# State-space stage of a two-layer backbone: phase sums and modulation weights moved to other stages, cosine in three steps, another order in the loop

## The chip, the core and the metric

The kernel runs on one core of a Trainium2 chip. The core has five engines that work side by side, each through its own list of instructions in order: TensorE (PE; loading of its weights is PEld), VectorE (DVE), ScalarE (ACT), GpSimd (POOL) and SyncE (SP). In this kernel SP issues every DMA transfer, so all transfers stand in one list. The metric is the time of one execution on the device, in microseconds (us).

## The reference

Two layers over 1024 latent tokens and 256 context tokens of width 1024, in float32. Layer 0 mixes tokens by differential attention, layer 1 by a bidirectional diagonal complex state-space recurrence (S5) with a GLU. A squared-ReLU MLP follows each mixer. Every sub-layer is normalized, and shifted, scaled and gated by "modulation" vectors: the product of SiLU(c) with a weight matrix of 1024 x 6144 for each layer, cut into six segments.

```python
def s5_scan(u, lam_bar, b_bar, c_mat, h0):              # per direction, 64 groups of 16 channels, 64 states
    ...
        bu = jnp.einsum('gpc,btgc->btgp', b_bar, uc.astype(jnp.complex64))
        a_cum, hs = lax.associative_scan(_linear_combine, (a, bu), axis=1)
        hs = hs + a_cum * h[:, None]
        y = jnp.real(jnp.einsum('gcp,btgp->btgc', c_mat, hs))
...
    def glu(y, h):
        g = jax.nn.gelu(y.astype(h.dtype))
        o1, o2 = jnp.split(jnp.einsum('btd,de->bte', g, w_glu), 2, axis=-1)
        return o1 * jax.nn.sigmoid(o2)
...
        mod_l = (jnp.einsum('bd,de->be', sc, ada_w[i]) + ada_b[i])[:, None, :]
        sh1, s1, g1, sh2, s2, g2 = jnp.split(mod_l, 6, axis=-1)
```

## The kernel before

Products that need float32 precision are made of three passes with split operands (`mm3`, L130 to L134: high by high, high by low, low by high), so most of the TensorE time stands on lines 132, 133 and 134. `split` (L136) makes the halves: ScalarE copies the high part, another engine subtracts for the low part. `dma` (L79) puts each transfer on SP.

In most stages a scheduler of the library sets the order of each engine's instructions and of SP's transfers, by its own estimate of times. Inside `manual` (L583) the order of PE, DVE, ACT and POOL is the program's own; SP's is still the scheduler's.

The stages that matter here, with their place in the profile:

- **First stage** (`phase_v`, L337, to about 245 us): modulation of layer 0, the V projection and the start of the K and Q projections. Beside it run, interleaved step by step, the remaining modulation segments of layer 0 (`ada`, products on L202) and `s5_prep` (L950), which prepares the state-space parameters. `s5_prep` also makes one phase step per state and direction, as a 32-bit integer turn, and stores it to DRAM (`phd`, L1018).
- **MLP of layer 0, second product** (`mlp0_down`, L1581): `s5_phases` (L1199) runs beside it. From the phase steps it fills by repeated doubling a fine table (16 positions) and a coarse table (10 positions of 16), and stores both (`ptd`).
- **State-space stage** (`s5`, L1735, about 1876 to 2101 us): 16 periods n, each for four channel groups in both directions d, over 160 positions at a time. A period's steps, all in `manual` order:
  - `phase` (L1773): POOL adds coarse and fine table to 640 integer phases (L1777).
  - `trig` (L1779): ScalarE makes sine and cosine. The cosine takes the sine of half the angle, a square, and a copy with scale -2 and bias 1: four instructions with the sine.
  - `inputs` (L1790, PE on L1797), `rotate` (L1799, two DVE multiplies on L1806), a POOL sum of both (L1887 or L1896), `scan` (L1813, on L1815), `back` (L1817, on L1823: one product on DVE, one on POOL), `outputs` (L1825, PE on L1829 and L1832).
  - the GELU two periods later (L1870 to L1904), and transposes of its result (`tr`, L1834), split in `tr_out` (L1838: the low half is L1841 on DVE).
  - eight half segments of layer 1's modulation: weights of 2 MB each are loaded into memory that the stage has freed, and multiplied in periods 8, 10 and 12 to 17 (`ada_half_products`, products on L247).
- **GLU** (`glu`, L1929, about 2102 to 2330 us): two groups g of four token tiles; for each of four column blocks nb, eight weight transfers and four tiles of 24 matmuls.

Three PSUM regions are shared by the input products of both directions, so that each product waits for the rotation of the third product before it. The outputs of a period are written to one of two banks, from which the GELU reads, and which the transposes then overwrite.

Of the kernel before, what the change touches and what calls it, by code (L numbers as in the profile page):

```python
# [70 lines left out]
class Prog:  # L71
# [265 lines left out]
    def phase_v(self):  # L337
# [48 lines left out]
        self.bg = [self.interleave([self.ada(0, seg, acc) for seg in (2, 3, 4)] + [self.rows_out(0, acc)],  # L386
# [15 lines left out]
        for nb in range(2):  # L402
            for n, (g, i) in enumerate(tok[4 * (1 - nb) :]):
# [16 lines left out]
                self.step(6 if nb and n else 7)  # L420
# [529 lines left out]
    def s5_prep(self):  # L950
# [67 lines left out]
        self.dma(self.phd, pc)  # L1018
# [180 lines left out]
    def s5_phases(self, o):  # L1199
# [3 lines left out]
        B, P, P16 = (self.fv(x, *d).bitcast(I32) for x, d in ((o, (128, 16)), (o + 8, (128,)), (o + 8.5, (128,))))  # L1203
        self.dma(self.fv(o + 9, 128), self.phd)
        nc.vector.tensor_copy(P, self.fv(o + 9, 128))
# [11 lines left out]
        fill(B, 16, P)  # L1217
        g(P16, B[:, :, 8], B[:, :, 8], ALU.add)
        self.dma(self.ptd[:, 5 * KB : 13 * KB], B.rearrange("p a b -> p (a b)"))
        yield  # L1220
        A = self.fv(o, 128, 10).bitcast(I32)
        fill(A, 10, P16)
        self.dma(self.ptd[:, 0 : 5 * KB], A.rearrange("p a b -> p (a b)"))
        yield
# [356 lines left out]
    def mlp0_down(self):  # L1581
# [6 lines left out]
        self.bg = [self.s5_phases(40), self.s5_tables(0, self.bank(3), self.bank(2))]  # L1588
# [146 lines left out]
    def s5(self):  # L1735
# [10 lines left out]
        At, Bt = self.fv(42.5, 128, 10).bitcast(I32), self.fv(47.5, 128, 16).bitcast(I32)  # L1746
        A0, B0 = self.hv(46, 2, 4, 10).bitcast(I32), self.hv(47, 2, 4, 16).bitcast(I32)
        phs = [(self.fv(x, 4, 160), self.fv(x + 2.5, 4, 160)) for x in (0, 7.5, 24.5)]
        ts = [[(self.fv(x, 4, 160), self.fv((12.5, 20)[d], 4, 160)) for x in ((5, 29.5), (15, 17.5))[d]] for d in range(2)]
# [9 lines left out]

        mods = [(6, 8), (8, 10), (10, 12), (11, 13), (12, 14), (13, 15), (14, 16), (15, 17)]  # L1760
        halves = [[self.view(self.U, 16 * i + 4 * kk, (2, 512)) for kk in range(4)] for i in range(2)]
# [11 lines left out]
        def phase(n, d):  # L1773

            x0, P = 64 * d + 4 * n, phs[(2 * n + d) % 3][0].bitcast(I32)
            a, b = (At[:, x0 : x0 + 4], Bt[:, x0 : x0 + 4]) if n else (A0[:, d], B0[:, d])
            pool.tensor_tensor(P.rearrange("p x (a b) -> p x a b", b=16), bcast(a, 3, 16), bcast(b, 2, 10), ALU.add)  # L1777

        def trig(n, d):  # L1779
            Ps, Pc = phs[(2 * n + d) % 3]  # L1780
# [3 lines left out]
            act.activation(Pc, Pc, AF.Copy, scale=-2.0, bias=1.0)  # L1784
# [14 lines left out]
        def rotate(n, d):  # L1799
            (Ps, Pc), (t1, t2) = phs[(2 * n + d) % 3], ts[d][n % 2]  # L1800
# [16 lines left out]
        def back(eng, n, d, j):  # L1817
            Ps, Pc = phs[(2 * n + d) % 3]
# [4 lines left out]
            eng.tensor_tensor(o, ts[d][n % 2][1][:, :, h], (Ps if j else Pc)[:, :, h], ALU.mult)  # L1823
# [19 lines left out]
        for t, c0, w in ((A0, 0, 10), (B0, 5 * KB, 16)):  # L1843
            self.dma(t, self.ptd[:, c0 : c0 + 128 * w].rearrange("p (d x w) -> p d x w", d=2, w=w)[:, :, 0:4])

        load_x(0)
        self.dma(self.fv(42.5, 13 * KB).bitcast(I32), self.ptd)
        load_w(0)
        self.act_set("silu_and_others")
        with self.manual():  # L1850
            act.activation(U[:, :, 160:192], U[:, :, 0:32], AF.Copy)
            for d in range(2):
                for i in range(2):
                    pool.memset(rs[d][i][:, :, 0:1], 0.0)
            phase(0, 0)
            phase(0, 1)
# [4 lines left out]
            for n in range(19):  # L1861
                run, m = n < 16, n - 2
                gelu = 0 <= m < 16
# [3 lines left out]
                if 1 <= n <= 16:  # L1867
                    back(pool, n - 1, 1, 1)
# [6 lines left out]
                if 0 < n < 15:  # L1875
                    phase(n + 1, 0)
                if run:
                    rotate(n, 0)
                if lo:
                    lo()  # L1880
                if gelu:
                    v.scalar_tensor_tensor(u, u, 1.0, y, ALU.add, ALU.mult)
                    act.activation(u, u, AF.Tanh, scale=float(np.sqrt(2.0 / np.pi)))
                if run:
                    inputs(n, 1)
                    t1, t2 = ts[0][n % 2]
                    pool.tensor_tensor(t1, t1, t2, ALU.add)  # L1887
                if gelu:
                    act.activation(u, u, AF.Copy, bias=1.0)
                if 0 < n < 15:  # L1890
                    trig(n + 1, 0)
                    decay(n + 1, 0)
                if run:
                    rotate(n, 1)
                    t1, t2 = ts[1][n % 2]
                    pool.tensor_tensor(t1, t1, t2, ALU.add)  # L1896
                    scan(n, 0)
                    if n == 0:
                        phase(1, 0)
                        trig(1, 0)  # L1900
                        decay(1, 0)
# [3 lines left out]
                if run:  # L1905
                    back(v, n, 0, 0)
                    back(pool, n, 0, 1)
                    scan(n, 1)
                    back(v, n, 1, 0)
                if 1 <= n <= 16:  # L1910
                    outputs(n - 1)
# [394 lines left out]
```

## Time and profile before

| what | us |
|---|---|
| runs of the kernel before | 2925.51, 2938.06, 2945.19 |
| their median | 2938.06 |
| span of the profiled execution, first to last instruction | 2929.2 |

The profiled execution has no time of its own beside its span; the median of the runs is 8.9 us above that span.

| stretch of the profile, us | PE busy | DVE | ACT | POOL | DMA share |
|---|---|---|---|---|---|
| 0 to 245, first stage | 205.96 | 113.54 | 74.18 | 54.06 | 0.81 |
| 1500 to 1870, MLP of layer 0 | 357.37 | 278.70 | 155.78 | 53.07 | 0.84 |
| 1870 to 1905, start of the state-space stage | 10.24 | 24.14 | 14.27 | 17.36 | 0.62 |
| 2075 to 2100, its end | 19.48 | 16.33 | 8.49 | 7.59 | 0.95 |

How to read the lines below: in a timeline a row gives start, duration, engine, source line, operation, output <- input, shape, and in brackets the idle time ahead of it with what ended it. SPq is SP's list of transfers. In a group of instructions stand the busy time, the mean of one in ns, and the idle time before them. Durations of matmuls overlap; what one costs is the step from one to the next.

### The profile page before, as it was taken

To read this page: it belongs to the slowest core of one execution; us is meant where nothing else is said; L and a number is where in the kernel's file an instruction comes from. 1 tells how busy PE (TensorE), PEld (TensorE's weight loads), DVE (VectorE), ACT (ScalarE), POOL (GpSimd) and SP (SyncE) were. 2 spreads that over 40 slices of the span, in tenths; PEclk is the share of its full clock that TensorE was granted. 3 is DMA by queue.
4 is the path that set the end of the run, shared out by engine and by line. 5 is a ranking of instruction groups with operands and counts; after the bars stand their busy time and mean duration, and the time that the engine had idled before them with its cause. 6 is when DMAs were issued, how large, how long until landed. Compare 5 with 4: busy or idle time off the path is not lost.

```text
span 2929.2 us, 43646 instructions
## 1 busy us (share of the span) xinstructions
PE 2739.6 (94%) x15200; PEld 2287.5 (78%) x15200; DVE 2021.3 (69%) x2956; ACT 1367.5 (47%) x2555; POOL 1062.1 (36%) x923
## 2 busy tenths in 40 slices
PE   5998999999988999999999999688899899999999
PEld 3687888788777887878877778588788678878887
DVE  5355777777764477676688768699743687758566
ACT  3424555555553663333444435377543643345443
POOL 2213666666553700000020004499410543326324
PEclk8999999999989999999999999899999999999999
DMA  9956455555744448886699988468834254467544
GB/s 250 292 181 205 139 164 169 162 149 162 220 145 152 140 152 303 303 291 243 228 299 293 274 241 258 153 200 264 282 124 136 72 175 159 148 213 256 159 139 141
DMA packets 454122, 588.44 MB, mean 201 GB/s; under 512 B 62742, under 2 KB 299532, under 8 KB 450700
## 3 DMA queue, kind: packets, MB, share of 16 engines
q1 hardware_dynamic: 453900, 585.63, 63.6%
q8 instruction: 120, 1.97, 0.3%
q14 instruction: 102, 0.84, 0.1%
HBM read 398.48 MB, written 182.82 MB: 198 GB/s over the span
## 4 chain that ended last, share of the span: by engine, by line
PE 66%; DMA 12%; DVE 10%; issue 4%; ACT 4%; SPq 2%; POOL 2%; DVEq 0%; ACTq 0%; POOLq 0%
PE PS L132 19%; PE PS L133 18%; PE PS L134 18%; SPq L80 2%; PE PS L520 2%; PE PS L1797 2%; ACT F L543 2%; PE PS L1832 1%; PE PS L566 1%; DVE F L533 1%; DVE R L138 1%; DVE H L138 1%; PE PS L202 1%; DMA U<-in_mlp_w 1%; DMA U<-Aa 1%
## 5 line engine op out<-in xcount | busy, mean ns | idle before, releaser
L132 PE MATMUL PS<-H 128*128 128x512 f32 x1048 | 412.0, 395 | 7.7 <-DVE FD L1604 5.0
L133 PE MATMUL PS<-H 128*128 128x512 f32 x1048 | 410.4, 392 | 0.0
L134 PE MATMUL PS<-H 128*128 128x512 f32 x1048 | 409.8, 392 | 0.0
L132 PE MATMUL PS<-H,R 128*128 128x512 f32 (+1 forms) x836 | 311.2, 378 | 18.5 <-ACT F L579 13.7
L133 PE MATMUL PS<-H,R 128*128 128x512 f32 (+1 forms) x836 | 303.8, 363 | 1.1 <-POOL H L138 1.1
L134 PE MATMUL PS<-H,R 128*128 128x512 f32 (+1 forms) x836 | 303.6, 364 | 0.0
L137 ACT ACTIVATE R<-W 128x512 fp32r<-128x512 f32 (+1 forms) x203 | 142.9, 711 | 208.7 <-PE PS L133 114.9
L132 PEld LDWEIGHTS PS<-H 128*128 128x128 f32 x1048 | 197.9, 189 | 52.4 <-DVE FD L1604 5.3
L134 PEld LDWEIGHTS PS<-H 128*128 128x128 f32 x1048 | 197.7, 189 | 42.5 <-issue 1.0
L133 PEld LDWEIGHTS PS<-H 128*128 128x128 f32 x1048 | 197.9, 189 | 41.2 <-issue 1.2
L132 PE MATMUL PS<-R,H 128*128 128x512 f32 x532 | 214.7, 407 | 7.4 <-ACT H L137 6.0
L543 ACT ACTIVATE F<-F,stat 128x1280 f32<-128x1280 f32 x128 | 174.3, 1362 | 83.8 <-DVE F L533 83.5
L133 PE MATMUL PS<-R,H 128*128 128x512 f32 x532 | 210.8, 397 | 0.0
L134 PE MATMUL PS<-R,H 128*128 128x512 f32 x532 | 208.3, 395 | 0.0
L137 ACT ACTIVATE H<-U 128x640 fp32r<-128x640 f32 x216 | 132.8, 677 | 144.2 <-PE PS L133 110.7
L132 PEld LDWEIGHTS PS<-H,R 128*128 128x128 f32 x836 | 160.7, 193 | 47.6 <-ACT F L579 15.1
L138 DVE TENSOR_TENSOR H<-W,H 128x512 fp32r<-128x512 f32 (+1 forms) x137 | 128.6, 949 | 93.6 <-ACT H L137 93.6
L138 DVE TENSOR_TENSOR R<-W,R 128x512 fp32r<-128x512 f32 (+1 forms) x166 | 150.8, 915 | 60.8 <-ACT R L137 53.5
L533 DVE TENSOR_SCALAR_CACHE_REDUCE F<-PS 128x1280 f32<-128x1280 f32 x128 | 185.1, 1482 | 9.1 <-PE PS L520 8.9
L138 DVE TENSOR_TENSOR H<-U,H 128x640 fp32r<-128x640 f32 x216 | 163.4, 793 | 39.5 <-ACT H L137 39.3
L580 POOL TENSOR_SCALAR R<-F 128x256 fp32r<-128x256 f32 (+1 forms) x128 | 122.8, 959 | 172.1 <-ACT F L579 149.1
L134 PEld LDWEIGHTS PS<-H,R 128*128 128x128 f32 x836 | 160.7, 192 | 25.9 <-issue 0.8
(477 smaller groups left out, 6818.0 us busy)
## 6 DMA issues: line engine op xcount, KB each, us to landing
W<-in_mlp_w SPq DMA_DIRECT2D x184, 256.0 KB, 3.1
U<-Aa SPq DMA_DIRECT2D x108, 320.0 KB, 5.0
Aa<-FU SPq DMA_DIRECT2D x91, 320.0 KB, 4.6
Ad<-F SPq DMA_DIRECT2D x112, 256.0 KB, 3.2
W<-Ad SPq DMA_DIRECT2D x112, 256.0 KB, 2.8
W<-in_ada_w SPq DMA_DIRECT2D x32, 512.0 KB, 6.9
FU<-in_mlp_w SPq DMA_DIRECT2D x32, 512.0 KB, 6.3
Ta<-FU SPq DMA_DIRECT2D x16, 1024.0 KB, 5.6
```

Of the source, the lines that this page charges most:

```text
L80: return self.nc.sync.dma_start(out=out, in_=in_)
L132: mm(out, ah, bh, start=first, stop=False, **kw)
L133: mm(out, ah, bl, start=False, stop=False, **kw)
L134: mm(out, al, bh, start=False, stop=last, **kw)
L137: self.nc.scalar.activation(hi, src, AF.Copy)
L138: (lo_eng or self.nc.vector).tensor_tensor(lo, src, hi.bitcast(F32), ALU.subtract)
L202: self.nc.tensor.matmul(acc[32 * j : 32 * j + 32, 0:256], self.scT[:, 2 * k : 2 * k + 32], w[:, 256 * j : 256 * j + 256], start=k == 0, st ...
L520: mm(self.PS[:, 1280 * c + k0 : 1280 * c + k1], Q[:, c, r, qs], K[c][:, k0:k1], start=r == 0, stop=r == 1)
L533: ts(p[c], self.PS[:, 1280 * c : 1280 * c + 1280], 1.0, None, ALU.mult, ALU.min, accum_out=sm[:, c : c + 1])
L543: nc.scalar.activation(p[c], p[c], AF.Exp, bias=sm[:, c : c + 1], scale=-1.0, accum_out=sn[:, 0:1] if c else s0[:, u + 1 : u + 2])
L580: nc.gpsimd.tensor_scalar(hi, t, 1.0, 0.0, ALU.mult, ALU.add)
L1797: mm(b[:, o : o + 160], X[:, d, i, 64 * j : 64 * j + 128], U[:, 4 * n + i, cols], start=True, stop=True)
```

## The change

Four edits.

1. `s5_phases` moves to the first stage, behind layer 0's modulation in the interleaved list, with memory of its own (`PH`, 14.75 KB per partition). It takes the phase steps from there, and not from DRAM, fills the tables for each direction, and adds them for all 16 periods: 32 sums of 128x640 on POOL, each stored to DRAM. The stage takes ten background steps where it took seven. In the state-space stage `phase` becomes a load of 320 KB; the two tables are not loaded any more.
2. The cosine is the sine of a quarter turn minus the absolute phase: with the sine three ScalarE instructions.
3. The order in a period: the scan of direction 1 moves behind the next period's first rotation, with its two products; POOL's sums, the low half and the GELU steps move with it. Phases have five buffers in place of three.
4. Layer 1's eight modulation halves leave the state-space loop. Each is multiplied in the GLU's first group after every second tile, from one set of four buffers that is loaded again after each; the modulation rows are written out after the second and the eighth.

```diff
-        self.bg = [self.interleave([self.ada(0, seg, acc) for seg in (2, 3, 4)] + [self.rows_out(0, acc)],
+        self.bg = [self.interleave([self.ada(0, seg, acc) for seg in (2, 3, 4)] + [self.rows_out(0, acc), self.s5_phases()],
...
-                self.step(6 if nb and n else 7)
+                self.step(10 if nb and n else 7)
...
-        self.dma(self.phd, pc)
+        v.tensor_copy(self.view(self.PH, 0, (128,)).bitcast(I32), pc)
...
+        out = Ring([i32(7.25 + 2.5 * i, 4, 10, 16) for i in range(3)])
...
+        for d in range(2):
+            fill(B, 16, P[:, 64 * d : 64 * d + 64])
+            g(P16, B[:, :, 8], B[:, :, 8], ALU.add)
+            fill(A, 10, P16)
+            yield
+            for n in range(16):
+                t, x = out.next(), slice(4 * n, 4 * n + 4)
+                g(t, bcast(A[:, x], 3, 16), bcast(B[:, x], 2, 10), ALU.add)
+                self.dma(self.phd[2 * n + d], t.rearrange("p x a b -> p (x a b)"))
+                yield
...
-        self.bg = [self.s5_phases(40), self.s5_tables(0, self.bank(3), self.bank(2))]
+        self.bg = [self.s5_tables(0, self.bank(3), self.bank(2))]
...
         def phase(n, d):
-            x0, P = 64 * d + 4 * n, phs[(2 * n + d) % 3][0].bitcast(I32)
-            a, b = (At[:, x0 : x0 + 4], Bt[:, x0 : x0 + 4]) if n else (A0[:, d], B0[:, d])
-            pool.tensor_tensor(P.rearrange("p x (a b) -> p x a b", b=16), bcast(a, 3, 16), bcast(b, 2, 10), ALU.add)
+            self.dma(phs[(2 * n + d) % 5][0].bitcast(I32).rearrange("p x n -> p (x n)"), self.phd[2 * n + d])
...
-            act.activation(Pc, Ps.bitcast(I32), AF.Sin, scale=0.5 * UNPHASE)
+            act.activation(Pc, Ps.bitcast(I32), AF.Abs, scale=UNPHASE)
             act.activation(Ps, Ps.bitcast(I32), AF.Sin, scale=UNPHASE)
-            act.activation(Pc, Pc, AF.Square)
-            act.activation(Pc, Pc, AF.Copy, scale=-2.0, bias=1.0)
+            act.activation(Pc, Pc, AF.Sin, scale=-1.0, bias=quarter)
```

The loop's new order, without its conditions (n is the period, m = n - 2 the one whose GELU is made):

```python
hi(n); square(m); trig(n, 1); decay(n, 1); inputs(n, 0); rotate(n, 0); decay(n + 1, 0)
scan(n - 1, 1); back(v, n - 1, 1, 0); back(pool, n - 1, 1, 1); add(n, 0); phase(n + 2, 0)
lo(); gelu step, tanh, plus 1; inputs(n, 1); rotate(n, 1); trig(n + 1, 0); outputs(n - 1)
scan(n, 0); back(v, n, 0, 0); back(pool, n, 0, 1); add(n, 1); gelu product
tr; phase(n + 2, 1); load_x(n + 2); load_w(n + 1)
```

And in the GLU:

```diff
-        for _ in self.rows_out(1, self.bank(3)):
-            pass
-        self.row_bc(G, 1, 2, 0)
+        halves = [(seg, h) for seg in (2, 3, 4, 5) for h in range(2)]
+        hw = [self.fv(16 + 4 * i, 2, 512) for i in range(4)]
+        self.ada_half_load(hw, 1, *halves[0])
...
+                    if g == 0 and t % 2:
+                        i = 2 * nb + t // 2
+                        self.ada_half_products(hw, 1, *halves[i], self.bank(5)[:, 0:128])
+                        if i < 7:
+                            self.ada_half_load(hw, 1, *halves[i + 1])
+                        if i in (1, 7):
+                            for _ in self.rows_out(1, self.bank(3)):
+                                pass
+                        if i == 1:
+                            self.row_bc(G, 1, 2, 0)
```

More of the change, by code (lines that the diff above doesn't have):

```diff
@@ L1745, in s5 @@
         rs = [[self.view(self.U, 52 + 5 * d + 2.5 * i, (4, 160)) for i in range(2)] for d in range(2)]
[L1746 to L1749, printed above, removed]
+        phs = [(self.fv(x, 4, 160), self.fv(x + 2.5, 4, 160)) for x in (0, 42.5, 7.5, 47.5, 24.5)]
+        quarter = self.fv(52.5, 1)
+        ts = [[(self.fv(x, 4, 160), self.fv(y, 4, 160)) for x, y in p]
+              for p in (((5, 12.5), (29.5, 53)), ((15, 20), (17.5, 20)))]
         cs = [[(self.fv(x, 4, 128), self.fv(y, 4, 128)) for x, y in (((5, 32), (29.5, 34)), ((15, 22.5), (17.5, 22.5)))[d]]
@@ L1874, in s5 @@
                     inputs(n, 0)
-                if 0 < n < 15:
-                    phase(n + 1, 0)
+                    rotate(n, 0)
+                if n + 1 < 16:
+                    decay(n + 1, 0)
+                if last:
+                    scan(n - 1, 1)
+                    back(v, n - 1, 1, 0)
+                    back(pool, n - 1, 1, 1)
                 if run:
-                    rotate(n, 0)
+                    add(n, 0)
+                if n + 2 < 16:
+                    phase(n + 2, 0)
                 if lo:
```

83 lines of the change are left out of this document (27 added, 56 removed).

## The prediction

> **What bounds the kernel now.** I read the page first, then the busy time by stretches, then one period of the state-space loop in order of time.
>
> ```profile
> span 2929.2 us, 43646 instructions
> ...
> PE 66%; DMA 12%; DVE 10%; issue 4%; ACT 4%; SPq 2%; POOL 2%; DVEq 0%; ACTq 0%; POOLq 0%
> ```
>
> TensorE carries two thirds of the chain that ended last. So matmuls added to a stage in which TensorE is full cost their whole length, and work on other engines counts only where TensorE waits for it. The stretches tell which stage is which (columns: PE, PEld, DVE, ACT, POOL busy, granted clock, DMA share, GB/s):
>
> ```profile
> 120.00:140.00 20.00, 19.98 (x138) 13.77 (x138) 8.52 (x12) 11.26 (x18) 2.88 (x4) 1.00 0.94 315
> 140.00:160.00 20.00, 20.00 (x116) 15.31 (x115) 8.74 (x10) 3.85 (x7) 3.78 (x3) 1.00 1.05 362
> 160.00:180.00 20.00, 20.00 (x103) 16.78 (x102) 7.20 (x15) 5.39 (x10) 1.69 (x3) 1.00 0.18 51
> 180.00:200.00 20.00, 20.00 (x109) 17.09 (x108) 17.15 (x50) 4.22 (x9) 4.31 (x4) 1.00 0.64 211
> 220.00:240.00 20.00, 12.84 (x66) 10.88 (x64) 2.95 (x5) 2.10 (x4) 1.29 (x1) 0.81 0.96 302
> ...
> 1905.00:2075.00 170.00, 149.94 (x1378) 143.57 (x1379) 164.26 (x160) 128.34 (x203) 160.25 (x87) 0.96 0.81 245
> ...
> 2100.00:2330.00 230.00, 218.70 (x973) 178.81 (x972) 104.82 (x123) 107.29 (x191) 50.31 (x51) 0.98 0.39 126
> ```
>
> The first stage (to 245) is full on TensorE with POOL nearly empty. The loop of the state-space stage (1905 to 2075) is the only place where DVE (164 of 170) and POOL (160) are full and TensorE is not. The GLU (2100 to 2330) is TensorE again, 95%, with DMA at 0.39. The change takes work from the second of these and puts it into the first and the third.
>
> **One period of the loop.** The two low halves (L1841) of neighbouring groups, 11.54 us apart, bracket a period without modulation:
>
> ```profile
> 1955.05 0.67 DVE L1841 SCALAR_TENSOR_TENSOR H<-PS,H 128x512 fp32r<-128x512 f32 x1
> ...
> 1955.64 0.67 DVE L1882 SCALAR_TENSOR_TENSOR FD<-FD,PS 128x512 f32<-128x512 f32 x1
> ...
> 1956.11 1.55 POOL L1887 TENSOR_TENSOR FD<-FD 128x640 f32<-128x640 f32 x1
> 1956.24 1.54 DVE L1806 TENSOR_TENSOR FD<-PS,FD 128x640 f32<-128x640 f32 x2
> ...
> 1957.70 1.49 DVE L1815 TENSOR_TENSOR_SCAN FD<-U,FD 128x640 f32<-128x640 f32 x1
> ...
> 1959.11 0.66 DVE L1904 TENSOR_TENSOR FD<-FD,PS 128x512 f32<-128x512 f32 x1
> ...
> 1960.34 0.60 PE L1836 MATMUL PS<-ident,FD 128*128 128x128 f32 x4
> ...
> 1960.78 3.43 PE L1797 MATMUL PS<-U,H 128*128 128x160 f32 x24
> 1961.02 2.56 DVE L1815 TENSOR_TENSOR_SCAN FD<-U,FD 128x640 f32<-128x640 f32 x1
> ...
> 1966.59 0.67 DVE L1841 SCALAR_TENSOR_TENSOR H<-PS,H 128x512 fp32r<-128x512 f32 x1
> ```
>
> The same scan takes 1.49 us and 2.56 us: the second starts while a POOL sum or product over SBUF is running. So DVE's full lane is partly waiting for POOL, and a POOL instruction taken away gives time to both.
>
> **Part 1: the loop.** Rows for the sum: the first rotations of groups 0, 1 and 15, of 8 and 9, the tail's pair of products, and the first GLU matmul.
>
> ```profile
> 1893.91 0.82 DVE L1806 TENSOR_TENSOR FD<-PS,FD 128x640 f32<-128x640 f32 x1 [0.82 <-PE PS L1797]
> 1905.99 1.56 DVE L1806 TENSOR_TENSOR FD<-PS,FD 128x640 f32<-128x640 f32 x2
> ...
> 1988.19 1.54 DVE L1806 TENSOR_TENSOR FD<-PS,FD 128x640 f32<-128x640 f32 x2
> ...
> 1999.63 4.51 PE L1797 MATMUL PS<-U,W 128*128 128x160 f32 x32
> 2000.99 0.82 DVE L1806 TENSOR_TENSOR FD<-PS,FD 128x640 f32<-128x640 f32 x1
> 2002.08 0.82 DVE L1806 TENSOR_TENSOR FD<-PS,FD 128x640 f32<-128x640 f32 x1 [0.26 <-PE PS L1797]
> ...
> 2074.93 1.55 DVE L1806 TENSOR_TENSOR FD<-PS,FD 128x640 f32<-128x640 f32 x2
> ...
> 2084.95 0.69 DVE L1823 TENSOR_TENSOR FD<-FD 128x512 f32<-128x512 f32 x1
> 2085.08 1.69 POOL L1823 TENSOR_TENSOR FD<-FD 128x512 f32<-128x512 f32 x1 [1.52 <-DVE FD L1815]
> ...
> 2102.94 2.08 PE L132 MATMUL PS<-R,H 128*128 128x512 f32 x4 [1.42 <-ACT R L137]
> ```
>
> From 1893.91 to 2074.93 the fifteen periods take 181.0. Removed: two POOL sums of phases per period. But the new order closes another ring. DVE now does rotation (n,0), scan (n-1,1), product, low half, GELU step, rotation (n,1), scan (n,0), product, GELU product; only then may TensorE transpose, since the transposes overwrite the bank that the GELU product reads; and the next group's input products stand behind the transposes. Measured from one rotation's start: its second multiply comes 1.09 later (2000.99 to 2002.08) and frees DVE after 0.73 (half of 1956.24 to 1957.70), 1.82; scan 1.49, 3.31; product 0.69, 4.00; low half and GELU step 0.59 and 0.60 (issue to issue, 1955.05, 1955.64, 1956.24), 5.19; rotation 1.46, 6.65; scan and product, 8.83; GELU product 0.66, 9.49; 0.44 from the transposes' start to the input products' (1960.34 to 1960.78), 9.93; 1.36 from those to the rotation (1999.63 to 2000.99), 11.29. With issue intervals (1.41 for the scan, 0.6 for the products) it is 11.0. POOL fits: its product ends 1.82 after the scan did (2085.08 plus 1.69, against 2084.95), its sum 1.55 later, 6.68, as the second rotation ends. I take 11.15, for twelve full periods. The first is 12.08 now (1893.91 to 1905.99), since group 1 waits for both scans; with the second scan behind the next rotation it is two rotations behind TensorE (4.1), scan and product, 6.3; I take 7, for products that wait for TensorE's slow start. Periods 2 and 3 lack the low half and some GELU steps: 10.3 each. Sum 7 + 20.6 + 133.8 = 161.4: **19.6 less**. Within the 181.0 are the periods that a modulation product lengthens (12.80 from 1988.19 to 2000.99); those go too.
>
> The tail from group 15's rotation to the GLU's first matmul is 28.0 (2074.93 to 2102.94). It loses three modulation blocks of TensorE (1.95 each, row below), and gains one scan with its products that now runs after the last rotation (1.49 + 1.82) and the low half in front of the outputs: I take **1 less**, between 4 less and 2 more.
>
> ```profile
> L1784 ACT ACTIVATE FD<-FD 128x640 f32<-128x640 f32 x29 | 21.4, 737 | 0.9
> ```
>
> The cosine's dropped ScalarE step is 0.74 a time, 32 times, but ScalarE (128 of 170) bounds no part of the ring: nothing. The price of the absolute value isn't in the trace; between this copy's 0.74 and double, ScalarE stays below the ring.
>
> **Part 2: the phases come by DMA.** 32 loads of 320 KB, queued on SP. The load for (n+2, 0) waits for POOL's product of (n-1, 1); behind it on SP stand group n+1's weights, wanted a period later. The trace has transfers of that size both ways:
>
> ```profile
> U<-Aa SPq DMA_DIRECT2D x108, 320.0 KB, 5.0
> Aa<-FU SPq DMA_DIRECT2D x91, 320.0 KB, 4.6
> ```
>
> Cover is more than a period (11), so nothing; without it a late load would cost its 5.0 once per period. The stage's traffic falls, since eight halves of 2 MB of modulation weights leave and 10.5 MB come.
>
> **Part 3: sums in the first stage.** POOL gets 32 sums of 128x640, and the table fills that it does today in the first layer's MLP, where they are on no path (leaving there: nothing).
>
> ```profile
> 1870.60 1.27 POOL L1777 TENSOR_TENSOR FD<-H 128x640 int32<-128x640 int32 x1 [0.46 <-DVE FD L1697]
> ```
>
> 32 x 1.27 = 41 us of POOL, which is at most a fifth busy in the slices from 120: it fits. The 32 stores are 10.5 MB, 29 us of transfer at the 362 GB/s of the slice from 140; the four slices from 120 leave 1.2 + 0 + 16.4 + 7.2 = 25. Half of them are queued before 160, where nothing is left, ahead of layer-one modulation weights (`W<-in_ada_w`) and V stores. SP is in order: behind each store that waits for POOL stand those, and behind them TensorE; the POOL queue also holds the rotary sums of K and Q. The wait of 7 at 220 to 240 for such K and Q loads shows that the end of the stage isn't covered. Bounds 0 and 15; I take **4 more**, nearer to 0 because the quiet slice from 160 can take most of it.
>
> **Part 4: modulation in the GLU.** Eight halves, each 64 matmul passes, a transpose, and four weight loads into one buffer set.
>
> ```profile
> 2092.32 1.95 PE L247 MATMUL PS<-U,scT 128*32 128x128 f32 x64
> ...
> 2109.06 0.39 PE L133 MATMUL PS<-R,H 128*128 128x512 f32 x1
> ...
> 2109.97 0.39 PE L134 MATMUL PS<-R,H 128*128 128x512 f32 x1
> ```
> ```profile
> 2083.37 3.09 SPq L80 DMA_DIRECT2D U<-in_ada_w  x4
> ```
> ```profile
> W<-in_ada_w SPq DMA_DIRECT2D x32, 512.0 KB, 6.9
> ...
> U<-in_ada_w SPq DMA_DIRECT2D x32, 512.0 KB, 9.4
> ```
>
> 8 x 1.95 = 15.6 on a full TensorE, with no idle time there to hide in. Transposes, in the changed program's order some twenty matmuls behind their products, so that no copy is waited for: about 0.15 each (0.60 for four, above), with the rows' own 1.5. The first loads can't start before the loop's memory is free, shortly ahead of the GLU's first matmul, and in the changed order the first eight products stand behind only four matmuls: 2.5, between 1 and 5. Each later set is loaded after its predecessor's products: issue 3.1 and landing 6.9 to 9.4 make 10.0 to 12.5, against 48 matmuls of 0.23 (four from 2109.06 to 2109.97), 10.9. So 0 to 1.6, seven times: 3, nearer to the 6.9, as this stage moves little. **22.6 more**, between 17 and 31. Behind a waiting load on SP stand the GLU's own weights.
>
> By the Trainium skill, page "DMA: Bandwidth & Descriptors", section "Anatomy of one DMA", a transfer costs about 2.0 us and its bytes over 436 GB/s, which for a half of 2 MB makes an estimate of 6.8 us: by it the matmuls would cover every reload, and the sum would be 3 lower. The trace's 6.9 for a quarter of that speaks against it.
>
> **Sum.** -19.6 - 1 + 22.6 + 4 = +6 on a span of 2929.2; the median is 8.9 above that span, and I carry that over: 2938 + 6 = **2944**.
>
> **The rivals.**
>
> *The loop gains little.* If a product of POOL goes ahead of DVE's each time (another 1.1 per scan), or the outputs are late for the input products, the period stays at 11.5 and only the start and the modulation go: 12 less instead of 20.6, so 2953. For it: my own two counts of the ring are 0.3 apart, and 11.29 is close to 11.54. Against it: the tail's rows show DVE first.
>
> *Slower: the store queue of the first stage.* A sum needs one of three buffers, whose store takes 4.6 to land, on an SP queue that waits for V evacuations and modulation products. If each store holds SP for over 1 us beyond its issue while TensorE waits for weights or V stores behind it, the 32 cost 32 us and not 4: 2972. It decides the sign of the verdict from about 0.9 per store. For it: DMA full from 120 to 160, TensorE in order. Against it: half of the stores come later.
>
> *Faster: both prices at their low ends.* The ring shrinks to DVE's own work, about 9.5 (1.46 + 1.49 + 0.69 + 0.59 + 0.60 + 1.46 + 1.49 + 0.69 + 0.66 is 9.1, with gaps), the GLU pays 17 and the first stage 0: -40 + 17, so 2915. Against it: the transposes do stand between GELU product and input products.
>
> *It doesn't do what it says: phases arrive late.* Each group then waits for its load, 5.0 in part: 16 x 2 more, 2976. Against it: the cover of over a period.
>
> **How the numbers follow.** About 1% (29 us) is what a measurement of this kernel can tell from no change. Chances: forecast 0.52 (2925 to 2958 by its bounds), little gain in the loop 0.22, store queue 0.12, late phases 0.04, faster 0.10. The range 2920 to 2967 takes the first two whole and leaves out most of the others. Slower by over 1%, above 2967: 0.12 + 0.04 and the upper ends of two bounds together, less the milder halves of the rivals: 0.14. Faster by over 1%, below 2909: 0.06, more than half of that rival staying above. The rest, 0.80, within 1%.
>
> **What would show it.** The rotations (L1803 now) of groups 4 to 15 at 11.0 to 11.3 apart, DVE waiting for TensorE in each; group 1's about 7 after group 0's; scans at 1.5 more often than 2.6; from 2100 a GLU longer by 17 to 31 with L247 in it eight times at 1.95, and any wait of L247 for `F<-in_ada_w`; waits of TensorE between 100 and 220, none today. Wrong would be: periods under 10.5 or over 11.7, the first stage longer by over 15, or a GLU that grows by less than its 15.6 of products.

## The result, and the profile after

The changed kernel takes **2962.8 us** (median of four runs, 2960.9 to 2966.65) against 2936.4 for the kernel before (four runs, 2925.5 to 2945.2): ratio 1.0094, 95% interval 1.0068 to 1.0120. That is some 26 us slower, inside the range of the prediction and 19 us above its forecast. The profiled execution took 2966.65.

Cutting both traces at the same five events shows where the time went. The events are the first matmul of the attention scores over all tokens (L520, end of the first stage; those over the context tokens, L514, come just ahead of it), the first rotations of groups 0 and 15, the first GLU matmul (L132) and the last tanh of the GLU (L1957, before L1961).

| stretch | before | after | difference | forecast |
|---|---|---|---|---|
| start to the first score matmul | 247.0 | 270.5 | +23.5 | +4 |
| from there to the first rotation | 1646.9 | 1647.1 | +0.2 | 0 |
| loop, rotation of group 0 to that of group 15 | 181.0 | 166.4 | -14.7 | -19.6 |
| tail, to the first GLU matmul | 28.0 | 29.4 | +1.4 | -1 |
| GLU, to its last tanh | 177.8 | 198.7 | +20.9 | +22.6 |
| the rest | 648.5 | 652.7 | +4.2 | 0 |

The differences add to 35.6 and not to 26, since the profiled execution of the kernel before was one of its fast ones and that of the changed kernel its slowest. The last row is no effect of the change: in the kernels below, which are all the same behind the GLU, that stretch lies between 646.3 and 653.2. The second row's stretch lies between 1638.6 and 1654.9 in them, so there a single profile is good to some us only. What the forecast missed is the first row.

**First stage.** The stretches of the changed kernel, with the columns as in the prediction:

```profile
140.00:160.00 20.00, 20.00 (x103) 14.79 (x103) 2.07 (x3) 1.79 (x3) 5.40 (x5) 1.00 1.02 355
160.00:180.00 20.00, 20.00 (x111) 15.93 (x110) 13.58 (x15) 3.85 (x7) 16.59 (x19) 1.00 0.90 291
180.00:200.00 20.00, 20.00 (x114) 17.18 (x113) 11.21 (x12) 7.18 (x13) 19.84 (x20) 1.00 0.59 218
...
240.00:260.00 20.00, 2.42 (x8) 1.86 (x8) 1.38 (x2) 0.63 (x1) 1.26 (x1) 0.51 1.00 346
...
1917.00:2084.00 167.00, 143.62 (x1093) 137.28 (x1092) 130.98 (x155) 108.64 (x168) 93.90 (x59) 0.98 0.72 228
2113.00:2343.00 230.00, 225.23 (x1434) 182.77 (x1434) 88.50 (x119) 97.58 (x182) 44.36 (x45) 0.98 0.57 193
```

The DMA share from 160 to 180 was 0.18 and is 0.90: the quiet slice filled up, as the prediction said, but for the most part not with the stores. Among the transfers issued in it are, before and then after:

```profile
Vd<-R SPq DMA_DIRECT2D x2, 256.0 KB
```
```profile
Vd<-R SPq DMA_DIRECT2D x8, 256.0 KB, 5.7
W<-in_attn_w_qkv SPq DMA_DIRECT2D x2, 512.0 KB, 4.8
phd<-PH SPq DMA_DIRECT2D x2, 320.0 KB
```

Two of the 32 phase stores start there; the rest is V's stores and projection weights, which went out earlier in the kernel before. POOL is full from 180 to 200. But TensorE now stands almost still from 240 to 260. Its waits up to 300 us name what is late (in total, times, longest):

```profile
PE PS L514 <- DMA R<-Kd: 18.4, 2, 18.1
...
PE PS L132 <- DVE R L462: 5.6, 1, 5.6
```

K is late: the scores over the context tokens wait 18.1 for its load, and behind them the next projection waits for DVE. The chain to K starts with three loads of projection weights in SP's list, in the kernel before:

```profile
141.34 4.87 SPq L80 DMA_DIRECT2D W<-in_attn_w_qkv  x2
153.05 1.35 SPq L80 DMA_DIRECT2D W<-in_attn_w_qkv  x1
```

and after:

```profile
151.79 0.38 SPq L80 DMA_DIRECT2D W<-in_attn_w_qkv  x1
165.75 0.37 SPq L80 DMA_DIRECT2D W<-in_attn_w_qkv  x1
167.65 0.39 SPq L80 DMA_DIRECT2D W<-in_attn_w_qkv  x1
```

The third is issued 14.6 later. Further down the list, the last store of K goes out 19.6 later (221.30 against 201.69) and its load 22.6 later (248.25 against 225.69). Between these stand transfers of Q and V and of the side work, so how much of the delay K's own weights carry is not shown. Until 236 TensorE still has other products to work on; the delay becomes a wait only when those are used up.

**Loop.** One period of the changed kernel, in order of time:

```profile
1993.01 0.82 DVE L1803 TENSOR_TENSOR FD<-PS,FD 128x640 f32<-128x640 f32 x1 [1.91 <-ACT FD L1868]
1994.03 0.82 DVE L1803 TENSOR_TENSOR FD<-PS,FD 128x640 f32<-128x640 f32 x1 [0.19 <-PE PS L1794]
1994.77 1.48 DVE L1812 TENSOR_TENSOR_SCAN FD<-U,FD 128x640 f32<-128x640 f32 x1
...
1997.64 0.49 PE L1826 MATMUL PS<-H,U 128*128 128x128 f32 x2 [1.47 <-DVE H L1838]
...
1999.66 1.49 DVE L1812 TENSOR_TENSOR_SCAN FD<-U,FD 128x640 f32<-128x640 f32 x1
...
2002.53 0.66 PE L1833 MATMUL PS<-ident,U 128*128 128x128 f32 x4 [0.16 <-DVE U L1904]
...
2003.02 4.51 PE L1794 MATMUL PS<-U,H 128*128 128x160 f32 x32
...
2004.38 0.82 DVE L1803 TENSOR_TENSOR FD<-PS,FD 128x640 f32<-128x640 f32 x1 [1.91 <-ACT FD L1868]
```

The period is 11.37 (1993.01 to 2004.38), both scans take 1.5, and DVE stands still for 1.91 before each first rotation. The wait is put down to a ScalarE instruction, but the rotation does not read its result; it follows the start of the input products by 1.36 (2003.02 to 2004.38), as it did in the kernel before (1999.63 to 2000.99). Those stand behind the transposes, which wait 0.16 for the GELU product: the ring of the prediction. TensorE itself has one long idle place, 1.47 before the outputs.

**GLU.** Two groups of TensorE's instructions between 2113 and 2312 (busy, mean ns, idle before):

```profile
L247 PE MATMUL PS<-F,scT 128*32 128x128 f32 x512 | 16.3, 279 | 0.5 <-DMA F<-in_ada_w 0.5
L254 PE MATMUL PS<-ident,adat 128*128 128x128 f32 x8 | 2.2, 271 | 0.0
```

The eight products are there in full, and all their loads together cost one wait of 0.5.

### The profile page after: what moved, and what is told of

Read it like the earlier page. It is cut to its first block, busy times and chain, and to the rows that moved or that the text cites. A ratio compares the mean times of both kernels' runs of the same rounds, so it can differ in the third digit from the quotient of the medians.

```text
span 2964.8 us, 43783 instructions
## 1 busy us (share of the span) xinstructions
PE 2749.6 (93%) x15201; PEld 2289.1 (77%) x15201; DVE 1984.4 (67%) x2957; ACT 1347.6 (45%) x2523; POOL 1041.4 (35%) x941
## 5 line engine op out<-in xcount | busy, mean ns | idle before, releaser
L132 PE MATMUL PS<-H 128*128 128x512 f32 x1048 | 412.0, 394 | 2.1 <-ACT H L137 1.6
L132 PE MATMUL PS<-H,R 128*128 128x512 f32 (+1 forms) x836 | 311.0, 377 | 23.3 <-ACT F L579 13.7
L1696 POOL TENSOR_TENSOR FD<-FD,W 128x1024 f32<-128x1024 f32 x3 | 11.6, 3895 | 714.5 <-DMA U<-Aa 714.5
L132 PEld LDWEIGHTS PS<-H 128*128 128x128 f32 x1048 | 197.6, 189 | 47.8 <-issue 4.8
L133 PEld LDWEIGHTS PS<-H 128*128 128x128 f32 x1048 | 197.8, 189 | 40.7 <-issue 0.8
L132 PE MATMUL PS<-R,H 128*128 128x512 f32 x532 | 215.1, 407 | 6.9 <-ACT H L137 5.2
L132 PEld LDWEIGHTS PS<-H,R 128*128 128x128 f32 x836 | 160.8, 193 | 52.4 <-ACT F L579 15.1
```

Source lines behind the costliest of these rows:

```text
L132: mm(out, ah, bh, start=first, stop=False, **kw)
L133: mm(out, ah, bl, start=False, stop=False, **kw)
L1696: pool.tensor_tensor(w, y, G, ALU.mult)
```

## The experiments

Each starts from the changed kernel, from the first experiment's, or from the kernel before; all medians are of four to ten runs beside runs of the kernel before (medians 2935.4 to 2937.6). The times by stage are read from the profiled execution, at the events of the table above.

| kernel | median, us | ratio to before (95%) | first score matmul | loop | tail | GLU |
|---|---|---|---|---|---|---|
| before | 2936.4 | | 247.0 | 181.0 | 28.0 | 177.8 |
| after | 2962.8 | 1.0068 to 1.0120 | 270.5 | 166.4 | 29.4 | 198.7 |
| sums_mlp | 2937.3 | 0.9975 to 1.0005 | 247.1 | 164.6 | 28.6 | 197.6 |
| no_stores | 2948.9 | 1.0011 to 1.0043 | 255.4 | 164.7 | 28.6 | 197.8 |
| no_sums | 2959.5 | 1.0038 to 1.0085 | 268.9 | 167.9 | 28.8 | 196.5 |
| stores_poolq | 2964.5 | 1.0045 to 1.0098 | 276.1 | 164.6 | 28.6 | 197.7 |
| step10 | 2938.6 | 0.9989 to 1.0030 | 247.8 | 168.3 | 29.3 | 197.9 |
| mods_gap | 2931.9 | 0.9965 to 0.9997 | 249.1 | 181.1 | 28.3 | 177.7 |
| inputs_first | 2926.9 | 0.9951 to 0.9986 | 247.9 | 157.6 | 28.8 | 196.5 |
| double_sums | 2950.0 | 1.0026 to 1.0059 | 249.2 | 181.8 | 29.4 | 196.9 |
| mods_bank | 2924.3 | 0.9930 to 0.9980 | 244.9 | 168.6 | 31.9 | 177.7 |
| best | 2926.1 | 0.9941 to 0.9978 | 249.9 | 167.3 | 29.3 | 177.7 |
| glu_only | 2946.1 | 1.0020 to 1.0052 | 249.3 | 175.0 | 26.4 | 196.9 |
| cosine_only | 2934.3 | 0.9978 to 1.0015 | 248.7 | 182.1 | 30.1 | 178.5 |

### sums_mlp: the sums in another stage

```diff
-        ... + [self.rows_out(0, acc), self.s5_phases()],
+        ... + [self.rows_out(0, acc)],
...
-                self.step(10 if nb and n else 7)
+                self.step(6 if nb and n else 7)
...
-        self.bg = [self.s5_tables(0, self.bank(3), self.bank(2))]
+        self.bg = [self.interleave([self.s5_tables(0, self.bank(3), self.bank(2))], [self.s5_phases(40)])]
...
-                self.step(2)
+                self.step(3)
```

The phase steps go through DRAM again, as in the kernel before, and the tables and buffers lie where its tables lay.

> The changed kernel, with the phase sums and their 32 stores taken out of the first stage (whose order of work is then that of the kernel before) and put into the first layer's MLP, second half. Theory A: the 23.8 us by which the first stage grew are the price of having sums and stores there, and the MLP hides them: 2963 - 24 = 2939, between 2934 and 2944, first rotation of the state-space loop back near 1894. Rival B: the price goes along, since TensorE is as full in the MLP and the loads of the MLP share the queue: 2955 to 2963.

2937.3, the first score matmul at 247.1 and the first rotation at 1894.2: theory A. The same 32 sums and 32 stores cost nothing beside the second product of the MLP. So the whole loss of the first stage is their place (with the table fills, which move along), and the other three edits together come out even with the kernel before.

### no_stores, no_sums, stores_poolq: what in the first stage costs

The edits of the loop over n in `s5_phases`, first no_stores, then no_sums, then stores_poolq:

```diff
-                self.dma(self.phd[2 * n + d], t.rearrange("p x a b -> p (x a b)"))
+                if n == 0:
+                    self.dma(self.phd[d], t.rearrange("p x a b -> p (x a b)"))
```
```diff
-                g(t, bcast(A[:, x], 3, 16), bcast(B[:, x], 2, 10), ALU.add)
+                if d == 0 and n < 3:
+                    g(t, bcast(A[:, x], 3, 16), bcast(B[:, x], 2, 10), ALU.add)
```
```diff
-                self.dma(self.phd[2 * n + d], t.rearrange("p x a b -> p (x a b)"))
+                nc.gpsimd.dma_start(out=self.phd[2 * n + d], in_=t.rearrange("p x a b -> p (x a b)"))
```

> The changed kernel with 30 of the 32 phase stores of the first stage left out (all sums stay; every load of the loop reads one of the two tiles stored). Theory A1, the queue: K's, Q's and V's transfers stand on SP behind stores that wait for POOL: 15 to 24 us less, 2939 to 2948. Theory A2, the port: POOL's sums slow DVE, whatever is stored: at most 5 less, 2958 to 2963. Theory A3, the volume: 10.5 MB more in a stage with full DMA: 15 to 24 less, as by A1.

> The changed kernel with 29 of the 32 phase sums left out (the tables and all 32 stores stay; the stores send the three tiles that were summed, so none waits for POOL but the first). A1, the queue: 15 to 24 us less, 2939 to 2948. A2, the port: the same, 2939 to 2948. A3, the volume: at most 5 less, 2958 to 2963.

> The changed kernel with the 32 phase stores issued by POOL, right behind its sums, instead of SP; sums, bytes and places are the same. A1, the queue: SP no longer waits for POOL, 15 to 24 us less, 2939 to 2948. A2, the port, and A3, the volume: no more than 5 less, 2958 to 2963; if the issue holds POOL for long, slower than that.

I had come out of the two traces with A1, the queue: after 183 us, SP issues eight phase stores one by one as POOL ends their sums, with the rotary swap of K behind them. SP does wait for POOL's sums there, 13.2 us in 14 waits between 100 and 250. But A1 falls as the price: with the stores off SP's list nothing is gained (2964.5), and without the sums, so that no store waits for POOL, only 3, less than these runs tell apart. Leaving the stores out gives 14 of the 25, just short of the 15 to 24 that A1 and A3 asked for. So what the stores bring is for the most part bytes, theory A3. Without the sums they are all sent early, and the transfers of the stretch read (first line the stretch 150 to 180, then SP's list):

```profile
150.00:180.00 30.00, 30.00 (x160) 22.38 (x159) 11.61 (x11) 3.50 (x7) 0.40 (x1) 1.00 1.02 343
```
```profile
171.96 0.38 SPq L80 DMA_DIRECT2D W<-in_attn_w_qkv  x1
180.69 0.37 SPq L80 DMA_DIRECT2D W<-in_attn_w_qkv  x1
184.39 0.64 SPq L80 DMA_DIRECT2D W<-in_attn_w_qkv  x1
```

The transfers are at 1.02 where the kernel before has 0.18 from 160 on, and the third load of weights goes out 31 us later than before. The delay of these weights does not give the price by itself: the first score matmul is 21.9 late here, but 23.5 in the changed kernel with its 14.6. Stores that go out in the same stage behind K's weights were not tried. In stores_poolq it is the same engines under another issuer (issued between 100 and 180):

```profile
phd<-PH POOLq DMA_DIRECT2D x16, 320.0 KB, 6.5
```

The Trainium skill says so in "DMA: Bandwidth & Descriptors", section "Issuing engines are not separate DMA queues": whichever engine starts a transfer, it runs on the same 16 DMA engines among all the others, and only the issuer's own time is saved. Runs and rule agree here.

POOL's work is the smaller part, 11.6 us by itself (no_stores against sums_mlp; 8.3 of it by the first score matmul). It is the sums and the table fills; no_sums keeps the fills too, and no run prices them alone. While POOL fills the tables, DVE's splits of the V weights in no_stores read

```profile
139.49 2.92 DVE L138 TENSOR_TENSOR R<-F,R 128x1024 fp32r<-128x1024 f32 x2 [0.70 <-ACT R L137]
142.33 3.31 DVE L138 TENSOR_TENSOR R<-FC,R 128x1024 fp32r<-128x1024 f32 x2
```

2.9 and 3.3 for two, against 1.23 for one, so 2.46 for two, in the kernel before:

```profile
130.37 1.23 DVE L138 TENSOR_TENSOR R<-F,R 128x1024 fp32r<-128x1024 f32 x1 [0.69 <-ACT R L137]
```

All eight such splits together take 2.0 longer than in the kernel before. The two prices do not add: 11.6 and 22.2 (no_sums against sums_mlp) alone, 25.5 together. Each contains the fills, and both delay the end of the same stage, though not by the same transfers: in no_sums the last store of K goes out 26.2 later than in the kernel before (228.51 against 202.35), while in no_stores it goes out 3.6 earlier (198.80) and only the loads behind Q's transfers come later (K's at 232.72, 7.0 later). What else than the splits makes up the 11.6, such as work behind the sums in POOL's own list, was not separated, and with each of these three edits the scheduler also laid the stage's order anew.

### step10: the pace of the side work

```diff
-                self.step(6 if nb and n else 7)
+                self.step(10 if nb and n else 7)
```

> The kernel of sums_mlp with the ten steps of side work per token block that the change brought to the first stage, without the sums and stores that it made room for. Theory: the steps alone cost nothing, 2934 to 2941. Rival: the 12 us by which no_stores stays above sums_mlp are the faster pace of the side work, not POOL's sums: 2946 to 2951.

2938.6: the faster pace costs nothing, so the 11.6 belong to the sums and the table fills.

### glu_only and cosine_only: single edits on the kernel before

In glu_only the loop's lines with `mods` are taken out of the kernel before, and the GLU is the changed kernel's. cosine_only is the kernel before with

```diff
-            act.activation(Pc, Ps.bitcast(I32), AF.Sin, scale=0.5 * UNPHASE)
+            act.activation(Pc, Ps.bitcast(I32), AF.Abs, scale=UNPHASE)
...
-            act.activation(Pc, Pc, AF.Square)
-            act.activation(Pc, Pc, AF.Copy, scale=-2.0, bias=1.0)
+            act.activation(Pc, Pc, AF.Sin, scale=-1.0, bias=quarter)
```

> The kernel before, with the modulation alone moved from the loop into the GLU. By the step sizes: the GLU 20 to 23 longer, the modulated periods of the loop (12.80 against 11.54) and the tail 7 to 12 shorter: 2937 + 12 = 2949, between 2945 and 2953. Rival: the loop's periods are set by DVE and POOL, so the loop gains below 4: 2954 to 2960.

> The kernel before, with the cosine in three steps alone. Theory: ScalarE bounds no part of the loop, no change: 2934 to 2940. Rival: ScalarE's chain stands in the ring, 0.74 per cosine or per group: 2913 to 2926.

Both times as expected. Moving the modulation costs 10.8 by the medians (9.9 if one of the ten runs, 8738 us long, is left out): the GLU is 19.1 longer, a little under the 20 expected, the loop 6.0 and the tail 1.7 shorter. The cosine does nothing (2934.3 against 2935.4). With sums_mlp this makes a ladder of medians from before to after: modulation +10.8, the loop's other edits -8.8 (2946.1 to 2937.3), first stage +25.5; 27.5 in all, where 26.4 was measured.

### double_sums: POOL's sums back in the loop

```diff
+        def double(n, d):
+            if 0 < n < 16:
+                t = phs[(2 * n + d) % 5][0].bitcast(I32)
+                pool.tensor_tensor(t, t, t, ALU.add)
...
                     add(n, 0)
+                    double(n + 1, 0)
...
                     add(n, 1)
+                    double(n + 1, 1)
```

> The kernel of sums_mlp with one POOL sum of 128x640 integers per direction and group put back into the state-space loop (each loaded phase is added to itself, so the phases are doubled); order, loads and all else stay. Theory P: it is the sums' absence that shortened the period, by freeing DVE's scans (1.49 against 2.56): 11.38 becomes 12.0 to 13.2, and the whole 2946 to 2965. Rival O: the new order did it and POOL has room: period below 11.6, 2936 to 2941.

2950.0, a period of 12.42 (below, 1985.49 to 1997.91) and a loop of 181.8, as long as that of the kernel before: theory P.

```profile
1985.49 0.82 DVE L1810 TENSOR_TENSOR FD<-PS,FD 128x640 f32<-128x640 f32 x1 [1.91 <-ACT FD L1875]
1985.59 1.25 POOL L1781 TENSOR_TENSOR FD<-FD 128x640 int32<-128x640 int32 x1
...
1987.25 1.48 DVE L1819 TENSOR_TENSOR_SCAN FD<-U,FD 128x640 f32<-128x640 f32 x1
...
1992.08 1.24 POOL L1781 TENSOR_TENSOR FD<-FD 128x640 int32<-128x640 int32 x1
1992.15 2.53 DVE L1819 TENSOR_TENSOR_SCAN FD<-U,FD 128x640 f32<-128x640 f32 x1
...
1997.91 0.82 DVE L1810 TENSOR_TENSOR FD<-PS,FD 128x640 f32<-128x640 f32 x1 [1.91 <-ACT FD L1875]
```

The sum at 1992.08 holds up the scan that begins 0.07 after it, by 1.05, and that is the whole difference of the period (12.42 against 11.37). The sum at 1985.59 starts while DVE multiplies out of PSUM, and holds up nothing. The kernel before needs its 181.0 with the modulation in the loop; without it, glu_only needs 175.0. So with POOL's sums at these two places the new order is 6.8 slower than the old one; the old order without the sums was not run. The Trainium skill, page "SBUF — State Buffer", section "Who interferes with whom", has a rule for this: a DVE instruction with two inputs in SBUF and a GpSimd instruction that reads SBUF contend for a read interface that they share, and the later one waits for the whole of the other. The scan and the rotation agree with it, the one with both large inputs in SBUF, the other with one in PSUM.

### inputs_first: the transposes out of the ring

```diff
                 if last:
                     outputs(n - 1)
+                if n + 1 < 16:
+                    inputs(n + 1, 0)
```

(and `inputs(n, 0)` at the top of the period only for n = 0)

> The kernel of sums_mlp with the next group's first input products ahead of the transposes instead of behind them. Theory, the ring of the prediction's Part 1: the transposes' place costs 0.65 in each period, so 11.38 becomes 10.7 and fourteen periods give 9: 2926 to 2931. Rival: another wait takes its place (the low half later, or DVE's own work), the period stays above 11.2: 2935 to 2939.

2926.9, 10.4 less, with these rows:

```profile
1962.06 2.34 PE L1796 MATMUL PS<-U,W 128*128 128x160 f32 x16
...
1963.42 0.82 DVE L1805 TENSOR_TENSOR FD<-PS,FD 128x640 f32<-128x640 f32 x1 [1.08 <-PE PS L1796]
1964.23 0.60 PE L1835 MATMUL PS<-ident,FD 128*128 128x128 f32 x4
...
1972.61 2.34 PE L1796 MATMUL PS<-U,H 128*128 128x160 f32 x16
...
1973.97 0.82 DVE L1805 TENSOR_TENSOR FD<-PS,FD 128x640 f32<-128x640 f32 x1 [1.08 <-PE PS L1796]
```

The period is 10.55; the input products still start 1.36 ahead of the rotation, DVE's wait falls from 1.91 to 1.08. The ScalarE instruction that the wait was put down to now ends 2.5 after the rotation's start, so it was not that one. So the ring that the prediction wrote out did set the period.

### mods_gap, mods_bank, best: the modulation back in the loop

mods_gap is sums_mlp with the GLU of the kernel before and, in the loop, products in the idle place that the period above shows (halves and loads as in the kernel before; the short work behind a product, `fin`, ahead of the transposes):

```diff
+                if n in mods:
+                    fin = self.ada_half_products(half(mods[n]), 1, 2 + mods[n] // 2, mods[n] % 2, self.PS[:, 1856:1984], later=True)
                 if last:
                     outputs(n - 1)
```

> The kernel of sums_mlp with the modulation taken out of the GLU and put back into the state-space loop, its products where TensorE waits 1.5 us per period for the low half, ahead of the outputs. Theory G, the gap: the GLU gives back 20 to 21, the loop takes 0.5 for each of eight products, the rows' own 1 to 2 come back: 2919 to 2925. Rival R1, the ring passes TensorE everywhere, so a product costs its whole 1.95 and some: 2931 to 2937. Rival R2, the 16.8 MB of weights make phases or group weights late: 2938 or more.

2931.9: at the lower edge of R1, but not by its mechanism. Rows of the products of groups 8, 10 and 12:

```profile
1983.40 1.95 PE L247 MATMUL PS<-U,scT 128*32 128x128 f32 x64 [2.79 <-DVE FD L1811]
2009.82 3.50 PE L247 MATMUL PS<-U,scT 128*32 128x128 f32 x64 [3.53 <-DVE FD L1811]
2034.18 1.95 PE L247 MATMUL PS<-U,scT 128*32 128x128 f32 x64
```

Two wait for the rotation of direction 1, the third for nothing. The three regions of the input products rotate, and in four of the eight groups that rotation reads the bank that holds the product's sum, though other columns of it. mods_bank takes the region that is free at that moment:

```diff
-                    ... self.PS[:, 1856:1984], later=True)
+                    ... xbank(n, 0, 1)[:, 832:960], later=True)
```

> The kernel of mods_gap with each product's sum in the PSUM bank that the running rotation does not read. In mods_gap the products of groups 8, 10, 13 and 14 waited 2.8 to 3.5 us for rotation (n,1), which reads the bank they write, and these periods were 14.3 to 16.6 long; the product of group 12, without that wait, left the period at 11.44. Theory G again: all eight fit the gap, four times 2.9 to 5.2 goes, 2913 to 2919. Rival R2, the transfers (DMA share 0.98 from 1960 to 2080): weights come late instead, 2923 to 2932.

> The kernel of mods_bank with the next group's first input products ahead of the transposes, as in inputs_first. Theory: the gains add, 2963 - 25 (sums out of the first stage) - 21 (modulation) - 10 (inputs first) = 2907, between 2903 and 2911. Rival: with shorter periods the transfers become the loop's bound, and the ten of inputs_first are not had again: 2912 to 2919.

2924.3 (the profiled execution took 2910.8). The loop is 12.5 shorter than in mods_gap (168.6 against 181.1), as theory G says, and a period with a product reads

```profile
1970.50 0.82 DVE L1811 TENSOR_TENSOR FD<-PS,FD 128x640 f32<-128x640 f32 x1 [1.91 <-ACT FD L1876]
...
1981.98 0.81 DVE L1811 TENSOR_TENSOR FD<-PS,FD 128x640 f32<-128x640 f32 x1
```

11.48 against 11.37 without: 1.95 us of matmuls for 0.1. Yet the median falls by 7.6 only, and ends in R2's range, though its nine runs spread over 26 us (2910.8 to 2936.9). The tail takes back 3.6 (31.9 against 28.3), and the transfers are at their limit (1960 to 2080):

```profile
1960.00:2080.00 120.00, 108.09 (x1233) 102.74 (x1231) 93.50 (x120) 71.36 (x117) 59.19 (x37) 0.97 1.03 335
```

The periods with a product are 11.4 to 11.5 long but for the last, 13.15: in it ScalarE waits 2.20 for a phase load, the modulation's copy comes late behind it, and TensorE waits 1.49 for that copy. In the tail the products wait 0.4 and the last outputs 1.7 for their weights. So the gap is free, and the transfers, phases among them, take a part of it back at the end.

best puts both together and gains nothing over either: 2926.1, loop 167.3, above the ranges of both its theory and its rival. Its periods with a product are 11.5 to 12.7 long, against 10.55 in the periods ahead of the first. In one of them:

```profile
1988.87 2.34 PE L1802 MATMUL PS<-U,W 128*128 128x160 f32 x16
...
1991.04 0.27 PE L255 MATMUL PS<-ident,adat 128*128 128x128 f32 x1
...
1991.35 0.17 DVE L257 TENSOR_TENSOR modc<-PS,modc 128x8 f32<-128x8 f32 x1 [2.97 <-PE PS L255]
...
1991.63 1.55 DVE L1811 TENSOR_TENSOR FD<-PS,FD 128x640 f32<-128x640 f32 x2
```

The rotation could start 1.36 after its input products, at 1990.23, but stands on DVE behind two small instructions of the modulation, and those wait for a transpose that my edit put on TensorE behind the input products: 1.4 lost. So the ten of inputs_first were not had again, as the rival said, but in this period by another cause than the transfers. Putting `fin` ahead of the input products was not tried. mods_bank, best and inputs_first all lie below the kernel before, by 0.3% to 0.5%.

## Why the prediction was right, and where it was not

The verdict (within 1%) and the range held, both narrowly and with luck: 2962.8 lies 4 below the upper end, and the one large error was just not large enough to leave the range. The sum behind the forecast held only in part.

**Part 3, the first stage, is the step that failed**: 4 taken, bounds 0 to 15, 23.5 in the trace and 25.5 by the runs; over 15 was the prediction's own sign of being wrong. The prediction counted DMA time that was left between 120 and 200 and concluded that "the quiet slice from 160 can take most of it". The slice did fill (0.18 to 0.90), but mostly with what the stores had pushed back. A slice is quiet because what it would carry had come before; 16 of the 32 stores went out between 100 and 180, most of them ahead of K's weights, which came 14.6 later, and the end of the stage was bare already in the kernel before (the wait of 7 for K and Q loads that the prediction names). The bounds treated the stores as a volume to be fitted in; the price was that of a delay ahead of the next stage. POOL's 41 us were called free because POOL was idle. With the table fills, also called free, they cost 11.6 by themselves.

The **rival of the store queue** priced this stage at 32 and came nearest in size, but its mechanism, SP held by stores that wait for POOL, is not what set the price: the waits are there (13.2), yet stores_poolq and no_sums, which take them away, gain nothing and 3.

**Part 1, the loop**: the ring was right in its parts. The row-by-row count said 11.29, the periods are 11.37 to 11.38; I had taken 11.15, which makes 2.7 of the missing 4.9 over twelve periods. Two more are the second period, 12.3 where 10.3 was assumed. About one of them is that its scan waits for POOL, and the first outputs for the product behind it:

```profile
1927.73 1.49 DVE L1812 TENSOR_TENSOR_SCAN FD<-U,FD 128x640 f32<-128x640 f32 x1 [1.22 <-POOL FD L1842]
...
1930.09 0.74 PE L1829 MATMUL PS<-H,FD 128*128 128x128 f32 x2 [2.24 <-DVE FD L1820]
```

The same two waits stand in sums_mlp, whose second period is 11.2. The other one is TensorE's granted clock: 0.57 in the changed kernel from 1930 to 1934, 1.00 at the same place in sums_mlp (1906 to 1910). Where a low clock lasts longer, as in step10 (0.54 and then 0.68, from 1905 to 1914), the second period is 14.1; this is most of what the same loop differs by in the table, 164.6 to 168.3. The first period was 7.3 (7 forecast). The tail is 1.4 longer, not 1 shorter, still inside its bounds. That the gain comes from the POOL sums that are gone, through DVE's scans, is shown by double_sums, and that no ScalarE wait sets the period by inputs_first; the cosine's nothing by cosine_only.

**Part 2, the phase loads**: in the changed kernel no wait for a phase appears on the way to a rotation. Right; with the modulation's weights back in the loop one does (mods_bank).

**Part 4, the GLU**: 20.9 (19.1 in glu_only) for 22.6. The products cost 16.3 for 15.6. The loads cost 0.5 where 2.5 for the first and 3 for the seven others stood; the remaining 4.1, with the transposes and rows, stood at 1.5. So two errors of opposite sign hide in the good total. I had read the landing of 6.9 for one of four transfers as speaking against the Trainium skill's estimate of 6.8 for the set ("DMA: Bandwidth & Descriptors", "Anatomy of one DMA"), which would have covered every reload. The trace sides with that result: the four transfers of a set overlap, so the landing of one is nearly that of all. From the second reload on they go out within 1.9 to 4.1 us, which with a landing of 6.5 (median) fits under 48 matmuls, 10.9. The section speaks of transfers that GpSimd issues; these are SP's.

## What to carry to other kernels

Before putting work on an idle engine or into a quiet stretch of the transfers, ask what is in order behind that stretch and how bare the wait at the stage's end already is: here bytes ahead of the next stage's first weights delayed its start by some twenty us, and the same bytes cost nothing in a stage with cover. A move costs what it adds where it lands, so test the landing place first: the same 32 sums and stores cost 25 us in one stage and none in another. Where a ring of waits is written out row by row, its longest gap on the full engine is a place for work: matmuls of 1.95 us cost 0.1 there, once their PSUM bank was not one in use.

## What I had not expected of the hardware

A product that writes columns of a PSUM bank waited up to 3.5 us for a DVE instruction that reads other columns of it, and choosing another bank took the wait away. In the trace the product is released by a semaphore that the DVE instruction raises, so the wait stands in the program; what the chip would do without it no run here shows.
